# A decoder layer on one core: the search's branch behind the searches, masks one after another, gating spread over ScalarE and GpSimd

## The chip, the core and the metric

The kernel runs on one core of a Trainium2 chip. A core has a matrix engine (TensorE, PE in the profile, with its weight loads shown apart as PEld), a vector engine (VectorE, DVE), an activation engine (ScalarE, ACT), a general engine (GpSimd, POOL) and a queue for transfers (SyncE, SP). Each takes its own instructions in a fixed order; they wait for each other by semaphores. The metric is the device time of one execution in microseconds (us).

## The reference, cut to what matters

One layer of a decoder, 1024 positions of 1024 channels, in float32. The norm of x is projected by W_in; its columns are shared by two mixers, whose outputs are normed, joined and projected by W_out; a feed-forward part of 4096 channels follows.

```python
# mixer A: 4 groups of 128 channels, chunks of 128 positions
z_u, z_v = gelu(p_u), gelu(p_v)
v = rms_norm(v by group, g_v)                  # v * (mean(v*v) + eps) ** -0.5 * g_v
out_A = u * (tril(w_s[g]) @ v_chunk + b_s[g])
# mixer B: 8 query heads of 64, 2 key heads; for each block of 128 queries
score = sum_h w[t,h] * relu(q_idx[t,h] . k_idx[s] / 8) ; non-causal scores = -inf
idx   = top_k(score, 256)                      # the keys that a query may see
o     = softmax(q . k / 8 over idx) @ v
# then
o = concat(rms_norm(out_A), rms_norm(o)) @ W_out
x = x + g1 * rms_norm(o); x = x + g2 * rms_norm(relu(h2 @ W_1) ** 2 @ W_2)
```

## The kernel before

Positions are cut into eight blocks of 128 (`NB`), the partitions of a tile. A float32 product is made of fp32r parts: `proj` runs three matmuls for each of eight slices of 128 channels, so that a projection of a block onto 512 columns is a group of 24 matmuls of 128x512 (L300 to L302) into one PSUM bank `p`.

The stages of the program are: modulation and norm of x; keys, values and index keys; for the blocks 7 to 2 the index queries and `index(b)`, which adds eight relu'd products into a score row `SC` (matmul L437, relu on ScalarE L438, sum on VectorE L441 and L442); mixer A's projections with `gating`; the query projections `q_proj`; the selection; attention with softmax; W_out; the feed-forward part.

`gating(cc, j, p)` runs 16 times, for two halves `cc` of the channels and eight blocks `j`, each one step behind its projection. ScalarE takes gelu of the 512 columns into `uv` (L505), the first 256 being u and the rest v, two groups of 128. VectorE sums the squares of each group into `ss` (L510). `rstd_of` makes the factor: scale and eps on VectorE (L98), power -0.5 on GpSimd (L99). VectorE multiplies v by the factor and by the gain row `gvb` into `vn` (L518). TensorE multiplies by the mask matrix `WM` (L519), and VectorE adds the bias and multiplies by u (L520).

The selection finds, for each of the blocks 7 to 2 (the others see at most 256 keys), the 256th largest score by bisection. `select(b)` counts in 15 steps how many 16-bit upper halves lie above a trial value. Blocks 6, 4 and 3 count with a sign on ScalarE (L597, followed by two one-column steps on VectorE, L598 and L599), 7, 5 and 2 on VectorE (L585, L587, L589). The eight largest of the lower halves among those that tie give the rest of the threshold. `search_rest` covers what these eight don't: VectorE sums a flag `more` over all blocks (L632), a matmul by `ones` sums it over the partitions (L634), VectorE copies it to an integer (L635), and a branch on VectorE (L637, L638) runs a second search if it is over zero. `mask(b)` then turns score and threshold into the row `BI` of zeros and huge values (L648 to L660: small threshold steps, compare, equals, a running sum over the ties, and two combining steps). Attention runs in units (b, group of four heads, pair of heads) in the order of the blocks `OB = (0, 7, 1, 6, 5, 4, 3, 2)`: `logits` multiplies (L704), VectorE adds `BI` and takes the extreme (L705), ScalarE takes the exponential (L708), `values` transposes and multiplies by V (L743, L729). Blocks 0 and 1 need no mask of the selection.

The order on each engine is set when the program is built: a scheduler with a simulated timeline takes, from the instructions whose inputs are ready by its own reckoning, the one with the lowest `tc.cur_priority`, which counts on from stage to stage (`stage(n)` sets it to n times 100000; the selection sets its own by `PRI`). PSUM has eight banks in three rings: `mm` with two, `tr` and `lg` with three each.

Of the kernel before, what the change touches and what calls it, by code (L numbers as in the profile page):

```python
# [16 lines left out]
OP = mybir.AluOpType  # L17
# [20 lines left out]
def trunk(ctx, tc, x, c, positions, w_ada, b_ada, g_pre_mix, w_in, g_sgu_v, w_spatial, b_spatial,  # L38
# [257 lines left out]
    def proj(p, j, wt, n, ks=range(KD)):  # L296
        h, t = hT[j // 4], (j % 4) * P
        for k in ks:
            lh, ll = h[:, 0, k, t:t + P], h[:, 1, k, t:t + P]
            T.matmul(p[:, :n], lh, wt[k][:, 0, :n], start=k == 0, stop=False)  # L300
            T.matmul(p[:, :n], lh, wt[k][:, 1, :n], start=False, stop=False)  # L301
            T.matmul(p[:, :n], ll, wt[k][:, 0, :n], start=False, stop=k == KD - 1)  # L302

# [199 lines left out]
    def gating(cc, j, p):  # L503
# [3 lines left out]
        ss = ssv[:, j, 2 * cc:2 * cc + 2]  # L507
        for i in range(2):
            v = uv[:, 256 + i * P:256 + (i + 1) * P]
            V.tensor_tensor_reduce(vn[:, i], v, v, scale=1.0, scalar=0.0, op0=OP.mult, op1=OP.add,  # L510
                                   accum_out=ss[:, i:i + 1])
        rstd_of(ss, ss, P)
        pg = p_mm()
        ya = up.tile([P, 2, P], F32, tag="ya", name=nm("ya"), bufs=2)
        for i in range(2):
            g = 2 * cc + i
            v = uv[:, 256 + i * P:256 + (i + 1) * P]
            V.scalar_tensor_tensor(vn[:, i], v, ss[:, i:i + 1], gvb[:, g * P:g * P + P], op0=OP.mult, op1=OP.mult)  # L518
            T.matmul(pg[:, i * P:(i + 1) * P], WM[:, g], vn[:, i], start=True, stop=True)  # L519
# [22 lines left out]
    def q_proj(b):  # L542
        p = p_mm()
        proj(p, b, wQ, 512)
# [4 lines left out]
    for b in OB:  # L549
        q_proj(b)  # L550
        if pend:
            last_gelu = gating(*pend.pop(0))
# [77 lines left out]
    def search_rest():  # L630
# [3 lines left out]
        T.matmul(p[:1, :1], more[:, 6:7], ones, start=True, stop=True)  # L634
        V.tensor_copy(rest, p[:1, :1])  # L635
        with tc.tile_critical():
# [6 lines left out]

    def mask(b):
        n = P * (b + 1)
        cnt, sg, kk, tf, kq, lf, top8, kd, th, lo, hi = ST[b]
        sc = score(b)
        V.tensor_copy(lo, lf)  # L648
# [4 lines left out]
        eq = up.tile([P, 1024], BF, tag="uv", name=nm("eq"), bufs=2)[:, :n]  # L653
        V.tensor_scalar(lt, sc, tf, None, op0=OP.is_lt, op1=OP.add, accum_out=cnt)
# [5 lines left out]
        V.scalar_tensor_tensor(lt, lt, -BIG, eq, op0=OP.mult, op1=OP.subtract)  # L660

    for b, pri in PRI:
        tc.cur_priority = pri
        select(b)

# [139 lines left out]
    for u, (b, grp, pair) in enumerate(units):  # L805
        if u == 3:
            search_rest()
            mask(7)
# [457 lines left out]
```

## Time and profile before

| | |
|---|---|
| median of 3 runs | 1272.2 us |
| lowest and highest run | 1265.81 and 1272.71 us |
| the profiled execution's own time | 1273.95 us |
| span of its trace | 1272.2 us |
| PE, DVE, ACT, POOL busy | 1171.3, 891.8, 644.5, 206.8 us |
| mean granted clock of TensorE | 0.959 of full speed |

A timeline row shows when an instruction started, how long it took, its engine and line, the operation, `out<-in` by the program's names, shapes and a count of equal neighbours; in brackets stands the idle time of the engine just before, and what ended it. On VectorE neighbouring small instructions overlap a little, so that a row's duration is somewhat more than the step to the next one. TensorE's rows overlap likewise: the step from matmul to matmul counts. A windows row gives for a stretch its length, the busy time and instructions of each engine, TensorE's granted clock, the share of the transfer engines and the data rate. A row of lines groups equal instructions: busy time in all and the mean of one in ns, then the idle time before them.

### The profile page before, as it was taken

What the parts mean: (1) busy time and instruction counts of PE and PEld (TensorE: products, weight loads), DVE (VectorE), ACT (ScalarE), POOL (GpSimd) and SP (SyncE); (2) the same over time, 40 slices, a digit from 0 to 9 for tenths busy, and PEclk for the clock granted to TensorE, in tenths of its full rate; (3) what the DMA queues carried; (4) which work ended last, traced back from release to release, by engine and by line L of the source; (5) the groups of instructions that cost most, each with busy time, mean ns of one, the idle gap of its engine ahead of it and who ended that gap; (6) DMA issues with size and microseconds to landing.
All of it is one profiled execution on the core that took longest, in us unless ns stands there. A gap on an engine that the chain in (4) does not pass through costs nothing.

```text
span 1272.2 us, 16825 instructions
## 1 busy us (share of the span) xinstructions
PE 1171.3 (92%) x5785; PEld 987.3 (78%) x5785; DVE 891.8 (70%) x1894; ACT 644.5 (51%) x1306; POOL 206.8 (16%) x280
## 2 busy tenths in 40 slices
PE   4889888889749999999889999999999899999997
PEld 4877677668639999878767878888888788888886
DVE  6833999987297656646898776556537846776668
ACT  4544557452327855545634555555544454445442
POOL 3675614132200000003630000000000000000001
PEclk9899999899759999989979999999999999999999
DMA  9420202010002124436404854344359355633335
GB/s 336 147 79 30 71 13 83 13 50 13 10 0 59 34 88 176 179 106 242 163 33 147 284 165 159 135 154 164 133 195 373 121 167 172 215 100 100 99 89 210
DMA packets 80240, 162.42 MB, mean 128 GB/s; under 512 B 7724, under 2 KB 32920, under 8 KB 80152
## 3 DMA queue, kind: packets, MB, share of 16 engines
q1 hardware_dynamic: 80136, 161.33, 37.7%
q8 instruction: 45, 0.74, 0.2%
q14 instruction: 43, 0.35, 0.1%
q10 hardware_dynamic: 16, 0.00, 0.0%
HBM read 119.36 MB, written 41.94 MB: 127 GB/s over the span
## 4 chain that ended last, share of the span: by engine, by line
PE 51%; DVE 12%; issue 4%; DMA 3%; ACT 1%; POOL 1%; SPq 0%; DVEq 0%; POOLq 0%; ACTq 0%
PE tr L1146 8%; PE lg L1146 8%; PE mm L1146 5%; PE mm L729 3%; PE lg L963 2%; PE lg L964 2%; PE lg L965 2%; DVE w L853 2%; PE tr L963 2%; PE tr L964 2%; PE tr L965 2%; PE tr L743 2%; PE lg L704 2%; PE mm L781 1%; PE mm L963 1%
## 5 line engine op out<-in xcount | busy, mean ns | idle before, releaser
L852 ACT ACTIVATE w<-rx 128x512 fp32r<-128x512 f32 x112 | 70.6, 630 | 148.5 <-PE lg L1146 61.2
L1146 PE MATMUL tr<-w,w 128*128 128x512 f32 x504 | 134.0, 391 | 3.8 <-DVE w L853 3.8
L1146 PE MATMUL lg<-w,w 128*128 128x512 f32 x504 | 133.7, 391 | 0.0
L300 PE MATMUL mm<-w,hT 128*128 128x512 f32 (+1 forms) x288 | 115.3, 401 | 9.8 <-ACT hT L293 3.8
L853 DVE TENSOR_TENSOR w<-rx,w 128x512 fp32r<-128x512 f32 x112 | 77.3, 690 | 58.9 <-ACT w L852 58.6
L1146 PEld LDWEIGHTS tr<-w,w 128*128 128x128 f32 x504 | 95.2, 189 | 24.0 <-DVE w L853 4.2
L302 PE MATMUL mm<-w,hT 128*128 128x512 f32 (+1 forms) x288 | 112.5, 391 | 0.9 <-POOL hT L294 0.9
L301 PE MATMUL mm<-w,hT 128*128 128x512 f32 (+1 forms) x288 | 112.5, 391 | 0.0
L1146 PEld LDWEIGHTS lg<-w,w 128*128 128x128 f32 x504 | 95.1, 189 | 19.8
L1182 POOL TENSOR_TENSOR rsf<-rsf,mhalf 128x1 f32<-128x1 f32 x8 | 6.0, 751 | 606.6 <-DVE rsf L1181 606.6
L1146 PE MATMUL mm<-w,w 128*128 128x512 f32 x336 | 94.3, 391 | 0.0
L729 PEld LDWEIGHTS mm<-VV,pT 128*128 128x128 f32 x576 | 74.3, 196 | 6.4 <-ACT pT L724 4.3
L729 PE MATMUL mm<-VV,pT 128*128 128x64 f32 x576 | 75.6, 275 | 2.9 <-ACT pT L724 2.9
L704 PE MATMUL lg<-KS,qs 128*128 128x512 f32 (+5 forms) x192 | 53.9, 394 | 24.2 <-DVE mxs L705 23.1
L300 PEld LDWEIGHTS mm<-w,hT 128*128 128x128 f32 x288 | 56.8, 197 | 21.5 <-ACT hT L293 4.0
L1146 PEld LDWEIGHTS mm<-w,w 128*128 128x128 f32 x336 | 63.2, 188 | 13.1
L853 DVE TENSOR_TENSOR w<-b,w 128x512 fp32r<-128x512 f32 x96 | 65.8, 686 | 4.5 <-ACT w L852 4.5
L302 PEld LDWEIGHTS mm<-w,hT 128*128 128x128 f32 x288 | 56.2, 195 | 10.9 <-POOL hT L294 1.2
L853 DVE TENSOR_TENSOR w<-s,w 128x512 fp32r<-128x512 f32 x56 | 38.2, 690 | 37.7 <-ACT w L852 37.7
L708 ACT ACTIVATE L<-L,mxs 128x128 f32<-128x128 f32 (+7 forms) x64 | 49.2, 770 | 30.0 <-DVE mxs L705 29.8
L301 PEld LDWEIGHTS mm<-w,hT 128*128 128x128 f32 x288 | 57.0, 198 | 8.9
L852 ACT ACTIVATE w<-b 128x512 fp32r<-128x512 f32 x96 | 59.3, 618 | 7.3 <-DMA b<-in_w_ff_dram 7.3
(356 smaller groups left out, 2969.5 us busy)
## 6 DMA issues: line engine op xcount, KB each, us to landing
rx<-x_scratch SPq DMA_DIRECT2D x56, 512.0 KB, 3.6
x_scratch<-d SPq DMA_DIRECT2D x108, 256.0 KB, 3.0
ada<-in_w_ada_dram SPq DMA_DIRECT2D x48, 512.0 KB, 6.0
raw<-in_w_ff_dram SPq DMA_DIRECT2D x32, 512.0 KB, 4.0
b<-in_w_ff_dram SPq DMA_DIRECT2D x32, 512.0 KB, 4.5
x<-in_x_dram SPq DMA_DIRECT2D x16, 512.0 KB, 5.6
raw<-in_w_in_dram SPq DMA_DIRECT2D x8, 512.0 KB, 3.5
raw<-in_w_in_dram SPq DMA_DIRECT2D x16, 256.0 KB, 2.8
```

The source lines that it names most:

```text
L300: T.matmul(p[:, :n], lh, wt[k][:, 0, :n], start=k == 0, stop=False)
L301: T.matmul(p[:, :n], lh, wt[k][:, 1, :n], start=False, stop=False)
L302: T.matmul(p[:, :n], ll, wt[k][:, 0, :n], start=False, stop=k == KD - 1)
L704: T.matmul(pl, QS[b, grp][:, q, h4 * P:(h4 + 1) * P], KS[:, grp, c0:c0 + cw], start=q == 0, stop=q == 1)
L708: ex = A.activation(L, L, AF.Exp, scale=-1.0, bias=top, accum_out=sms[:, b, h:h + 1])
L729: mm = T.matmul(po[:, o:o + 64], e[:, (si * 2 + h2) * P:(si * 2 + h2 + 1) * P], VV[:, s0 + si, grp], start=first, stop=pair == 1 and s0 + ...
L852: A.activation(hi, src, AF.Copy)
L853: eng.tensor_tensor(lo, src, hi.bitcast(F32), op=OP.subtract)
L963: ms.append(T.matmul(p, a[:, 0, k], b[:, 0, k], start=start and k == 0, stop=False, skip_group_check=more))
L964: ms.append(T.matmul(p, a[:, 0, k], b[:, 1, k], start=False, stop=False, skip_group_check=more))
L965: ms.append(T.matmul(p, a[:, 1, k], b[:, 0, k], start=False, stop=stop and k == 3, skip_group_check=more))
L1146: ms.append(T.matmul(p, x[:, qa, t * P:(t + 1) * P], y[:, qb], start=start and n == 0, stop=stop and n == 2, skip_group_check=more))
```

## The change

In the gating, the sum of squares goes to ScalarE (Square with an accumulator), and so does the multiplication by the factor (Copy with a scale for each partition). The product of v and the gain row becomes a GpSimd instruction of 128x256 in place. The factor's two steps both run on GpSimd. The bank of the mixing product comes from the ring `tr`, not from `mm`; the two mixing matmuls are written ahead of the two last VectorE steps. In the selection, `search_rest` and `mask(7)` are written directly behind the searches with a priority of their own, where they stood behind the third attention unit. The last two query projections, of blocks 3 and 2, are made in `search_rest` and ordered behind the flag's matmul. The masks are chained: the compare's predecessor tells a mask to start behind the end of the one before it.

```diff
@@ -295,11 +295,14 @@
 
     def proj(p, j, wt, n, ks=range(KD)):
         h, t = hT[j // 4], (j % 4) * P
+        first = None
         for k in ks:
             lh, ll = h[:, 0, k, t:t + P], h[:, 1, k, t:t + P]
-            T.matmul(p[:, :n], lh, wt[k][:, 0, :n], start=k == 0, stop=False)
+            mm = T.matmul(p[:, :n], lh, wt[k][:, 0, :n], start=k == 0, stop=False)
+            first = first or mm
             T.matmul(p[:, :n], lh, wt[k][:, 1, :n], start=False, stop=False)
             T.matmul(p[:, :n], ll, wt[k][:, 0, :n], start=False, stop=k == KD - 1)
+        return first
 
     def rope(t, j, nh, pool):
 
@@ -505,18 +508,20 @@
         ge = A.activation(uv, p, AF.Gelu_apprx_tanh)
         vn = up.tile([P, 2, P], F32, tag="vn", name=nm("vn"), bufs=2)
         ss = ssv[:, j, 2 * cc:2 * cc + 2]
+        v = uv[:, 256:512]
         for i in range(2):
-            v = uv[:, 256 + i * P:256 + (i + 1) * P]
-            V.tensor_tensor_reduce(vn[:, i], v, v, scale=1.0, scalar=0.0, op0=OP.mult, op1=OP.add,
-                                   accum_out=ss[:, i:i + 1])
-        rstd_of(ss, ss, P)
-        pg = p_mm()
+            A.activation(vn[:, i], v[:, i * P:(i + 1) * P], AF.Square, accum_out=ss[:, i:i + 1])
+        G.tensor_tensor(v, v, gvb[:, 256 * cc:256 * cc + 256], op=OP.mult)
+        G.tensor_scalar(ss, ss, 1.0 / P, EPS, op0=OP.mult, op1=OP.add)
+        G.tensor_tensor(ss, ss, mhalf[:, :2], op=OP.pow)
+        for i in range(2):
+            A.activation(vn[:, i], v[:, i * P:(i + 1) * P], AF.Copy, scale=ss[:, i:i + 1])
+        pg = p_tr()
         ya = up.tile([P, 2, P], F32, tag="ya", name=nm("ya"), bufs=2)
         for i in range(2):
+            T.matmul(pg[:, i * P:(i + 1) * P], WM[:, 2 * cc + i], vn[:, i], start=True, stop=True)
+        for i in range(2):
             g = 2 * cc + i
-            v = uv[:, 256 + i * P:256 + (i + 1) * P]
-            V.scalar_tensor_tensor(vn[:, i], v, ss[:, i:i + 1], gvb[:, g * P:g * P + P], op0=OP.mult, op1=OP.mult)
-            T.matmul(pg[:, i * P:(i + 1) * P], WM[:, g], vn[:, i], start=True, stop=True)
             V.scalar_tensor_tensor(ya[:, i], pg[:, i * P:(i + 1) * P], cols[:, 72 + g:73 + g],
                                    uv[:, i * P:(i + 1) * P], op0=OP.add, op1=OP.mult)
         A.activation(vn.rearrange("p a b -> p (a b)"), ya.rearrange("p a b -> p (a b)"), AF.Square,
@@ -539,14 +544,14 @@
     QT = {}
     OB = (0, 7, 1, 6, 5, 4, 3, 2)
 
-    def q_proj(b):
+    def q_proj(b, behind=None):
         p = p_mm()
-        proj(p, b, wQ, 512)
+        after(proj(p, b, wQ, 512), behind)
         QT[b] = qp.tile([P, 512], F32, tag="q", name=nm("q"), bufs=8)
         A.activation(QT[b], p, AF.Copy)
         rope(QT[b], b, 8, qp)
 
-    for b in OB:
+    for b in OB[:6]:
         q_proj(b)
         if pend:
             last_gelu = gating(*pend.pop(0))
@@ -631,8 +636,10 @@
 
         V.tensor_scalar(more[:, :6], KDS, 8.0, None, op0=OP.is_gt, op1=OP.add, accum_out=more[:, 6:7])
         p = p_tr()
-        T.matmul(p[:1, :1], more[:, 6:7], ones, start=True, stop=True)
+        flag = T.matmul(p[:1, :1], more[:, 6:7], ones, start=True, stop=True)
         V.tensor_copy(rest, p[:1, :1])
+        for b in OB[6:]:
+            q_proj(b, flag)
         with tc.tile_critical():
             r = V.value_load(rest)
             with V.If(r > 0):
@@ -641,27 +648,34 @@
                     search(BI[:, boff[b]:boff[b] + P * (b + 1)].bitcast(U16), 15, lf, cnt, kd, kk, V.drain)
                 V.drain()
 
+    masked = [None]
+
     def mask(b):
+
         n = P * (b + 1)
         cnt, sg, kk, tf, kq, lf, top8, kd, th, lo, hi = ST[b]
         sc = score(b)
-        V.tensor_copy(lo, lf)
+        first = V.tensor_copy(lo, lf)
         V.scalar_tensor_tensor(th, hi, 16, lo, op0=OP.logical_shift_left, op1=OP.bitwise_or)
 
         V.tensor_tensor(tf, th.bitcast(F32), sg, op=OP.mult)
         lt = BI[:, boff[b]:boff[b] + n]
         eq = up.tile([P, 1024], BF, tag="uv", name=nm("eq"), bufs=2)[:, :n]
+        after(first, masked[0])
         V.tensor_scalar(lt, sc, tf, None, op0=OP.is_lt, op1=OP.add, accum_out=cnt)
         V.tensor_scalar(eq, sc, tf, BIG, op0=OP.is_equal, op1=OP.mult)
         V.tensor_tensor_scan(sc, eq, eq, 0.0, op0=OP.add, op1=OP.max)
         V.tensor_scalar(cnt, cnt, float(TOPK - n), BIG, op0=OP.add, op1=OP.mult)
         V.tensor_tensor(cnt, cnt, sc[:, n - 1:n], op=OP.add)
         V.scalar_tensor_tensor(eq, sc, cnt, eq, op0=OP.is_gt, op1=OP.mult)
-        V.scalar_tensor_tensor(lt, lt, -BIG, eq, op0=OP.mult, op1=OP.subtract)
+        masked[0] = V.scalar_tensor_tensor(lt, lt, -BIG, eq, op0=OP.mult, op1=OP.subtract)
 
     for b, pri in PRI:
         tc.cur_priority = pri
         select(b)
+    tc.cur_priority = 465000
+    search_rest()
+    mask(7)
 
 
     stage(6)
@@ -803,9 +817,6 @@
     logits(0)
     stack_for(2)
     for u, (b, grp, pair) in enumerate(units):
-        if u == 3:
-            search_rest()
-            mask(7)
         if u + 1 < len(units):
             logits(u + 1)
         values(u)
```

The line numbers of the profile before move a little: of the places named below, L300, L301 and L302 become L301, L303 and L304; L437 becomes L440, L519 L522, L634 L639, L319 L322, L704 L718, L705 L719, L380 L383, and the mask's lines L648 to L660 become L658 to L671.

The first place is TensorE's order where the index ends. `lg_...<-KI` is the last product of the index scores of block 2, `mm_...<-w,hT` a projection group, `<-vn,WM` a gating's mixing product. Before:

```order
L437 MATMUL lg_1668<-KI,qs_1651 128x384 x2
L437 MATMUL lg_1674<-KI,qs_1651 128x384 x2
L437 MATMUL lg_1680<-KI,qs_1651 128x384 x2
L519 MATMUL mm_2209<-vn_2204,WM 128x128
L300 MATMUL mm_2219<-w_2060,hT_142 128x512
```

After:

```order
L440 MATMUL lg_1674<-KI,qs_1651 128x384 x2
L303 MATMUL mm_1978<-w_1732,hT_143 128x512
L304 MATMUL mm_1978<-w_1732,hT_143 128x512
L301 MATMUL mm_1978<-w_1735,hT_143 128x512
L303 MATMUL mm_1978<-w_1735,hT_143 128x512
L304 MATMUL mm_1978<-w_1735,hT_143 128x512
L440 MATMUL lg_1680<-KI,qs_1651 128x384 x2
L522 MATMUL tr_1970<-vn_1962,WM 128x128 x2
L301 MATMUL mm_2021<-w_1705,hT_143 128x512
```

Behind the last index product there were 13 projection groups to come (five of mixer A and all eight of the queries); now there are 17 (nine and eight), of which 15, with 12 pairs of mixing products among them, stand ahead of the flag.

The second place is the flag on TensorE. `more` and `ones` are its operands, `hT_143` and `hT_142` the second and first half of the positions. Before, the flag stood among the last pieces of block 0's attention:

```order
L704 MATMUL lg_3863<-KS,qs_3202 128x512 x2
L729 MATMUL mm_3224<-VV,pT_3228 128x64 x2
L683 MATMUL tr_3239<-ident,ya_3232 128x128 x4
L634 MATMUL tr_3247<-ones,more 1x1
L743 MATMUL tr_3872<-ident,L_3212 128x128
L743 MATMUL tr_3872<-ident,L_3218 128x128
L319 MATMUL tr_3884<-ident,qd_3882 128x128 x4
```

After (the 48 matmuls of the two last query projections are cut to the first and the last):

```order
L304 MATMUL mm_2659<-w_2473,hT_143 128x512
L639 MATMUL tr_3073<-ones,more 1x1
L301 MATMUL mm_3076<-w_2446,hT_142 128x512
...
L304 MATMUL mm_3109<-w_2473,hT_142 128x512
L322 MATMUL tr_3753<-ident,qd_3751 128x128 x4
L718 MATMUL lg_3761<-KS,qs_3750 128x128
```

The flag now stands behind the sixth query projection and ahead of the last two, and block 0's first transposes and logits come behind those.

The third place is the masks on VectorE, directly behind the branch. `self_` and `seli_` hold a block's search values, `SC` its scores; tiles of 1024 columns are block 7's, of 896 block 6's, of 768 block 5's, of 640 block 4's. Before, the six masks went through one another:

```order
L654 TENSOR_SCALAR BI,self_2766<-SC,self_2766 128x1024
L655 TENSOR_SCALAR eq_3844<-SC,self_2766 128x1024
L649 SCALAR_TENSOR_TENSOR seli_2757<-seli_2757 128x1
L654 TENSOR_SCALAR BI,self_2764<-SC,self_2764 128x896
L655 TENSOR_SCALAR eq_3959<-SC,self_2764 128x896
L654 TENSOR_SCALAR BI,self_2762<-SC,self_2762 128x768
L654 TENSOR_SCALAR BI,self_2760<-SC,self_2760 128x640
...
L656 SCALAR_TENSOR_TENSOR SC<-eq_3844 128x1024
```

After, from the end of mask 7 to the first softmax step of block 0:

```order
L671 SCALAR_TENSOR_TENSOR BI<-BI,eq_3736 128x1024
L658 CAST seli_2715<-self_2714 128x1
...
L665 TENSOR_SCALAR BI,self_2714<-SC,self_2714 128x896
L666 TENSOR_SCALAR eq_3975<-SC,self_2714 128x896
...
L670 SCALAR_TENSOR_TENSOR eq_3975<-SC,self_2714,eq_3975 128x896
L383 TENSOR_TENSOR qs_3750<-tr_3753,qs_3750 128x512
L671 SCALAR_TENSOR_TENSOR BI<-BI,eq_3975 128x896
L658 CAST seli_2713<-self_2712 128x1
L719 ISA L_3760,mxs<-lg_3761,BI 128x128
```

Mask 7 and then mask 6 now run whole, and both stand ahead of block 0's first softmax step; of mask 5 the first half stands between that step and block 7's first softmax step, and the masks 4 to 2 come later still.

## Rows read from the trace of the kernel before

**Rows 1.** The page's first line.

```profile
span 1272.2 us, 16825 instructions
```

**Rows 2.** Windows: three stretches; the last columns are clock, DMA share, GB/s.

```profile
135.20:245.20 110.00, 98.42 (x453) 80.49 (x453) 104.86 (x312) 65.83 (x147) 34.54 (x40) 0.95 0.14 40
...
350.00:400.00 50.00, 31.66 (x211) 27.41 (x212) 48.26 (x112) 24.02 (x46) 3.28 (x2) 0.73 0.11 30
400.00:450.00 50.00, 48.86 (x397) 46.92 (x397) 30.51 (x95) 37.86 (x83) 4.70 (x8) 1.00 0.10 29
```

**Rows 3.** Timeline of VectorE from the end of the searches on.

```profile
318.01 0.16 DVE L632 TENSOR_SCALAR_CACHE_REDUCE more<-kds 128x6 f32<-128x6 f32 x1
...
329.77 0.69 DVE L380 TENSOR_TENSOR qs<-tr,qs 128x512 fp32r<-128x512 f32 x1 [10.83 <-ACT qs L379]
...
343.34 0.15 DVE L635 CAST rest<-tr 1x1 int32<-1x1 f32 x1 [3.08 <-PE tr L634]
348.39 0.34 DVE L648 CAST seli<-self 128x1 int32<-128x1 f32 x4 [4.91 <-DVEq L636]
...
366.44 0.69 DVE L705 CUSTOM_DVE_ANT_0 L<-lg,BI 128x512 f32<-128x512 f32 x1
```

**Rows 4.** Timeline of TensorE: end of the index, block 0, block 7.

```profile
240.16 0.62 PE L437 MATMUL lg<-KI,qs 128*128 128x384 f32 x2 [0.20 <-ACT relu L438]
...
328.40 0.60 PE L319 MATMUL tr<-ident,qd 128*128 128x128 f32 x4
...
344.21 0.66 PE L729 MATMUL mm<-VV,pT 128*128 128x64 f32 x4
367.19 1.22 PE L704 MATMUL lg<-KS,qs 128*128 128x512 f32 x2 [22.32 <-DVE mxs L705]
```

**Rows 5.** Timeline of ScalarE: copies at the ends of two query projections.

```profile
317.71 0.60 ACT L546 ACTIVATE q<-mm 128x512 f32<-128x512 f32 x1 [4.84 <-PE mm L302]
323.15 0.60 ACT L546 ACTIVATE q<-mm 128x512 f32<-128x512 f32 x1 [4.84 <-PE mm L302]
```

**Rows 6.** Lines by form: VectorE's steps of mask 7, from 340 to 372.

```profile
L656 DVE TENSOR_TENSOR_SCAN SC<-eq 128x1024 f32<-128x1024 bf16 x1 | 2.3, 2292 | 0.0
...
L659 DVE SCALAR_TENSOR_TENSOR eq<-SC,self,eq 128x1024 bf16<-128x1024 f32 x1 | 1.3, 1284 | 0.0
L654 DVE TENSOR_SCALAR_CACHE_REDUCE BI<-SC,self 128x1024 bf16<-128x1024 f32 x1 | 1.3, 1278 | 0.0
L660 DVE SCALAR_TENSOR_TENSOR BI<-BI,eq 128x1024 bf16<-128x1024 bf16 x1 | 1.2, 1224 | 0.0
...
L655 DVE TENSOR_SCALAR eq<-SC,self 128x1024 bf16<-128x1024 f32 x1 | 0.8, 755 | 0.0
```

**Rows 7.** Timeline of VectorE: end of the index, a gating's steps, neighbours of GpSimd.

```profile
245.04 0.62 DVE L442 SCALAR_TENSOR_TENSOR SC<-relu,WI,SC 128x384 f32<-128x384 f32 x1
...
258.19 0.29 DVE L510 CUSTOM_DVE_ANT_0 vn<-uv 128x128 f32<-128x128 f32 x1
...
258.62 0.15 DVE L589 SCALAR_TENSOR_TENSOR self<-self 128x1 f32<-128x1 f32 x1
...
260.07 0.61 DVE L518 SCALAR_TENSOR_TENSOR vn<-uv,ssv,gvb 128x128 f32<-128x128 f32 x2
...
263.23 0.35 DVE L520 SCALAR_TENSOR_TENSOR ya<-mm,cols,uv 128x128 f32<-128x128 f32 x1
...
276.59 0.94 DVE L599 SCALAR_TENSOR_TENSOR self<-self 128x1 f32<-128x1 f32 x1
277.46 2.72 DVE L518 SCALAR_TENSOR_TENSOR vn<-uv,ssv,gvb 128x128 f32<-128x128 f32 x2
```

**Rows 8.** Timeline of GpSimd at the last two rows of that.

```profile
276.22 3.81 POOL L222 TENSOR_TENSOR w<-raw,w 128x512 fp32r<-128x512 f32 x3
```

**Rows 9.** Lines by form, whole run: GpSimd and ScalarE operations of 128x256.

```profile
L294 POOL TENSOR_TENSOR hT<-hf,hT 128x256 fp32r<-128x256 f32 x8 | 6.1, 760 | 3.5 <-DVE hf L291 1.8 <-ACT hT L293 1.7
...
L522 ACT ACTIVATE vn<-ya 128x256 f32<-128x256 f32 x16 | 6.7, 416 | 5.2 <-DVE ya L520 5.2
```

## The prediction

> **What bounds the kernel now.** I read the windows first. From 400 us on TensorE is the bound: 48.86 of 50 us busy at full clock [rows 2]. Whatever makes its work start sooner before 400 comes off the end one for one, unless other work is pushed behind 400. In the 50 us before, it is different: TensorE is busy for 31.66 at a mean clock of 0.73, and VectorE for 48.26 [rows 2]. So that stretch is VectorE's, and the timeline of VectorE tells why. The searches are over at 318.01 with the sum `more`. VectorE then stands idle for 10.83 us until 329.77, where it starts on block 0; the flag reaches it only at 343.34, behind 3.08 us of waiting for TensorE; the branch costs 4.91 us of idle time; the masks start at 348.39, and block 7's first softmax step is at 366.44 [rows 3]. TensorE, which finished the query projections at 328.40 and block 0's work at about 344.87, waits 22.32 us for that step [rows 4]. The reader is to see two holes that stand one behind the other: VectorE waits for TensorE from 318 to 330, and TensorE waits for VectorE from 345 to 367. They could lie beside each other if the flag came first.
>
> Further ahead, from 135 to 245 us, VectorE is busy for 104.86 of 110 us and TensorE for 98.42 [rows 2]: there the index sums and the searches on VectorE set the pace. TensorE's last index product is at 240.16 [rows 4], VectorE's last index sum at 245.04 [rows 7].
>
> **Behind the flag.** Call F the time at which TensorE runs the flag's matmul. The steps that follow are all in VectorE's order: copy and branch, from 343.34 to 348.39, 5.05 us [rows 3]. Mask 7: the five wide steps take 2.29, 1.28, 1.28, 1.22 and 0.76, together 6.83 [rows 6]; five one-column steps stand in the chain as well, most hidden behind their neighbours, for which I take 0.7: 7.5. Mask 6 has 896 columns, seven eighths of 6.83 is 6.0, with the small steps and one subtraction of block 0 of 0.69 [rows 3] in it about 7.2. So VectorE is through at F+19.8. Meanwhile TensorE makes the two last query projections, 5.44 us each by the step between their copies [rows 5], until F+10.9; it then has only block 0's first transposes and logits, so a hole of some 8 us remains on TensorE.
>
> Block 0 then runs as before: from VectorE's start on it at 329.77 to where VectorE began to wait for the flag, 343.34 less 3.08, is 10.5 us [rows 3]. The first half of mask 5, some 3 to 4 us of VectorE, stands in this piece; the old piece was full of waits, so I let it hide. That gives block 7's first softmax step at F+30.3, with 27 as the low bound (block 0's first logits and transposes already lie behind the masks) and 33 as the high one (the mask 5 work doesn't hide). What VectorE still owes to the later masks at that point is about the same as before: there, the compares of all masks were done, here the running sum of mask 5 is done instead. So I give nothing back later.
>
> **Where F falls.** F is set by TensorE. A matmul of a group takes 5.44 / 24 = 0.227 us [rows 5]. Behind the last index product there are now 15 groups ahead of the flag, 360 matmuls, 81.8 us, and 12 pairs of mixing products of about 0.3, 3.6 us: 85.4. Before, 13 groups, 70.9 us, and some 2 us of mixing products took from 240.8 to 328.4, 87.6 us [rows 4], so 15 us were lost in waits and low clock there. Much of that was the bank of the mixing product, which stood in the ring of two that the projections use and was let go only when VectorE, busy with searches, had done L520. With the bank in another ring I take 6 us of loss for the new stretch. So F is 91.4 us behind the last index product.
>
> That product comes earlier by what VectorE is relieved of, since VectorE is the bound of that stretch. A gating had on VectorE two sums of squares, 0.43 (258.19 to 258.62), two scalings, 0.61, and one factor step of about 0.15 [rows 7]. By the old order eleven gatings had their sums of squares and ten their scalings ahead of 245.04, of sixteen; now all this is off VectorE: 11 x 0.43 + 10 x 0.6 = 10.7 us. By the new order also some four to five gatings stand behind the index that stood ahead of it, each with a pair of L520, of 0.35 each and overlapped, about 0.5 [rows 7]: 2.3. Together 13 us off.
>
> Against this stands GpSimd's new product of v and the gain. No row has it; the nearest is another 128x256 product there, 0.76 us [rows 9]. Its price for VectorE is shown by a row: while three GpSimd products of 128x512 ran for 3.81 us from 276.22 on, a one-column step that takes 0.15 otherwise took 0.94, and a pair of scalings that takes 0.61 took 2.72 [rows 7, 8]. About seven of the new products fall into the stretch. The low bound is nothing (each falls into an instruction that isn't held), the high one 7 x 0.76 = 5.3 us; a VectorE instruction in the middle of such a product waits for half of it on average, 2.7 us, which I take, as the squares and scalings that were held worst are gone from VectorE.
>
> The Trainium skill ("SBUF — State Buffer", section "🔬 SBUF: two separate sides") says that GpSimd and certain VectorE instructions share a pair of ports under an exclusive lock and that the later one blocks fully until the other is done. The stretched rows at 276 us agree. By this rule alone all sixteen products would cost VectorE 12 us, and the gain on VectorE would be nearly used up; by the rows the cost is about half, because only an instruction already at the door is held.
>
> ScalarE gets four instructions for each gating. The nearest row is a square of 128x256, 0.416 us, with its accumulator read [rows 9]; two of half the width and two copies I estimate at 1.2 us, seven times 1.2 is 8 us on 65.83 of 110 [rows 2]. It has room on the mean; in its order they stand among the index relus and the signs.
>
> So the last index sum moves from 245 to 245 - 13 + 2.7, about 234.5 (range 230 to 245), TensorE's last index product to about 229.5, and F to 229.5 + 91.4 = 321. A second way agrees: TensorE does the same work ahead of F as it did ahead of 328.40, less two projections, so with equal waits F would be 328.4 - 10.9 = 317.5; it gets more waits during the index, where 23 us of projections no longer fill its holes, and fewer behind. VectorE is not what F waits for: it was ready at 318 and is relieved of all 16 gatings, 16 x 1.04 = 17 us, of which locks take back about 6, while the searches with signs, whose ScalarE now also has the squares, may lose up to 10: ready between 307 and 317.
>
> **The sum.** Block 7's first step at 321 + 30.3 = 351.3 instead of 366.44: 15.1 us earlier. The profiled execution took 1273.95 us with a span of 1272.2 [rows 1]; less 15.1 this is 1258.9. The median of the runs is 1.75 us below that execution; the lowest of them lies 6 us below the median, so I don't shift for it: 1259.
>
> **The rivals.** A stronger one: the index ends at 230 on VectorE and TensorE loses only 2 us in the stretch behind. Then F is 225.5 + 87.4 = 313, and with 27 us behind it block 7 starts at 340, 26 us earlier: 1248. For it speaks that VectorE's load was the whole delay; against it that TensorE still has all its work.
>
> No change: the index ends where it did, as the locks take 5 us and ScalarE's squares and copies, which wait for one another and for GpSimd's power within a gating, hold up the relus that stand behind them. Then F is 240.5 + 91.4 = 332, and block 7 starts at 362: 4 us earlier, 1270, which is within 0.5%, that is 6.4 us, about what runs of this kernel can tell. For it speaks that ScalarE's order is strict and that the profile shows waits of TensorE for relus even now (0.20 at the last index product [rows 4]); against it the 44 us of room on ScalarE.
>
> Slower: ScalarE becomes the bound of the index. Its copies in a gating wait for the square, the factor and the power on GpSimd, with the product of 0.76 ahead of them there, and every relu behind them waits too; TensorE's ring of three index banks then runs full. This decides from the point where F + 30.3 passes 366.4, so F 336, the last index product at 244.7 and VectorE's last sum at 249. If it ends at 251 and the 15 us of old waits stay, F is 246.5 + 85.4 + 15 = 347, block 7 at 377, 11 us later: 1285.
>
> **How the numbers follow.** Forecast (F between 314 and 329, gain of 7 to 22 us, 1252 to 1267): 0.60. Stronger: 0.12. No change: 0.20. Slower: 0.08. The range leaves out the slower case and the far ends, and goes from the stronger case's time less a little to that of no change: 1245 to 1270. Faster by over 0.5% means under 1265.8: the stronger case and nearly all of the forecast, with a twentieth taken from it for the part with F over 327 and a little of the no-change case given back, 0.72. Within: 0.20. Slower: 0.08.
>
> **What would show it.** In the trace after: the last index sum on VectorE near 234 and not 245; the flag near 321 with no bank waits in the stretch ahead of it; an idle VectorE ahead of the flag's copy, which shows that TensorE sets F; the two last query copies within 12 us behind the flag; mask 7 in one piece of 7 to 8 us; block 7's first step 27 to 33 us behind the flag; TensorE idle some 8 us between the last query projection and block 0 instead of 22 ahead of block 7; from 400 on the same picture, 15 us earlier. Stretched one-column steps on VectorE beside the gain products would show the lock. The prediction is wrong if the index ends at 245 or later, if VectorE and not TensorE is late at the flag, or if block 7's wait for its mask returns as a wait of equal length in block 0 or in the blocks behind.

## The result, and the profile after

The changed kernel takes 1255.84 us (median of 6 runs, 1254.35 to 1258.13); the one before took 1271.49 on the same chip. The ratio is 0.9888, with an interval of 0.9863 to 0.9912: faster by 1.1%, 15.7 us. The profiled execution took 1255.87 us, 18.1 less than the profiled one before.

First the windows of the changed kernel: length, busy time of PE, PEld, DVE, ACT and POOL, then TensorE's clock, DMA share and GB/s.

```profile
135.20:245.20 110.00, 94.48 (x409) 76.37 (x408) 104.67 (x281) 78.42 (x202) 40.04 (x54) 0.88 0.13 38
160.00:190.00 30.00, 21.19 (x81) 16.13 (x80) 29.93 (x78) 18.99 (x44) 2.33 (x4) 0.74 0.00 1
...
350.00:400.00 50.00, 46.18 (x338) 42.31 (x338) 43.80 (x124) 35.79 (x76) 4.27 (x7) 0.93 0.16 48
400.00:450.00 50.00, 50.00 (x400) 48.34 (x399) 27.37 (x84) 36.08 (x74) 2.91 (x5) 1.00 0.06 17
```

Against [rows 2]: the stretch from 350 to 400 now has TensorE busy for 46 us instead of 32. From 135 to 245 TensorE does less than before, and from 160 to 190 it is starved, at a clock of 0.74. The kernel before did more there:

```profile
160.00:190.00 30.00, 26.77 (x127) 22.40 (x126) 29.86 (x98) 18.23 (x42) 5.51 (x6) 0.94 0.04 14
```

The timeline of VectorE of the changed kernel, at the points of [rows 3] and [rows 7]: last index sum, end of the searches, flag's copy, start of mask 7, first softmax steps of block 0 and of block 7.

```profile
224.20 1.30 DVE L445 SCALAR_TENSOR_TENSOR SC<-relu,WI,SC 128x384 f32<-128x384 f32 x1
...
306.68 0.15 DVE L637 TENSOR_SCALAR_CACHE_REDUCE more<-kds 128x6 f32<-128x6 f32 x1
...
316.47 0.15 DVE L640 CAST rest<-tr 1x1 int32<-1x1 f32 x1 [8.88 <-PE tr L639]
325.43 0.15 DVE L658 CAST seli<-self 128x1 int32<-128x1 f32 x1 [8.81 <-DVEq L643]
...
341.15 0.28 DVE L719 CUSTOM_DVE_ANT_0 L<-lg,BI 128x128 f32<-128x128 f32 x1
...
348.60 0.69 DVE L719 CUSTOM_DVE_ANT_0 L<-lg,BI 128x512 f32<-128x512 f32 x1 [0.20 <-PE lg L718]
```

Block 7 starts at 348.60 instead of 366.44, 17.8 us earlier. The end of the index came 20.8 us earlier and the end of the searches 11.3; but VectorE then stood idle for 8.88 us until TensorE reached the flag, and for 8.81 in the branch, where it had been 4.91.

TensorE's timeline has the last index product, the flag, and the hole that is left behind the last query projection:

```profile
221.06 0.52 PE L440 MATMUL lg<-KI,qs 128*128 128x384 f32 x2
...
316.24 0.19 PE L639 MATMUL tr<-ones,more 128*1 128x1 f32 x2
...
340.23 0.91 PE L718 MATMUL lg<-KS,qs 128*128 128x128 f32 x3 [8.77 <-DVE qs L383]
```

The 22.32 us of [rows 4] have become 8.77, ahead of block 0, where masks 7 and 6 stand on VectorE.

### The profile page after: what moved, and what is told of

It is laid out like the page before. It is cut to its first block, busy times and chain, and to the rows that moved or that the text cites. A ratio compares the mean times of both kernels' runs of the same rounds, so it can differ in the third digit from the quotient of the medians.

```text
span 1254.1 us, 16871 instructions
## 1 busy us (share of the span) xinstructions
PE 1169.4 (93%) x5785; PEld 987.7 (79%) x5785; DVE 876.2 (70%) x1782; ACT 661.9 (53%) x1402; POOL 222.9 (18%) x312
## 4 chain that ended last, share of the span: by engine, by line
PE 60%; DVE 7%; issue 3%; DMA 1%; POOL 1%; ACT 1%; DVEq 0%; POOLq 0%; SPq 0%; ACTq 0%
PE lg L1157 9%; PE tr L1157 9%; PE mm L1157 6%; PE mm L743 5%; PE lg L974 3%; PE lg L975 3%; PE lg L976 3%; PE tr L974 3%; PE tr L976 3%; PE tr L975 3%; PE tr L757 2%; PE lg L718 2%; PE mm L974 2%; PE mm L975 2%; PE mm L976 2%
## 5 line engine op out<-in xcount | busy, mean ns | idle before, releaser
L301 PE MATMUL mm<-w,hT 128*128 128x512 f32 (+1 forms) x288 | 113.2, 394 | 7.9 <-ACT hT L293 3.4
L304 PE MATMUL mm<-w,hT 128*128 128x512 f32 (+1 forms) x288 | 111.4, 388 | 1.0 <-POOL hT L294 1.0
L303 PE MATMUL mm<-w,hT 128*128 128x512 f32 (+1 forms) x288 | 111.7, 388 | 0.0
L301 PEld LDWEIGHTS mm<-w,hT 128*128 128x128 f32 x288 | 56.2, 195 | 18.6 <-ACT hT L293 3.6
L304 PEld LDWEIGHTS mm<-w,hT 128*128 128x128 f32 x288 | 55.7, 194 | 10.4 <-POOL hT L294 1.3
L303 PEld LDWEIGHTS mm<-w,hT 128*128 128x128 f32 x288 | 56.2, 195 | 8.5
L718 PE MATMUL lg<-KS,qs 128*128 128x512 f32 (+5 forms) x192 | 53.3, 388 | 10.2 <-DVE qs L383 8.8
```

The lines of the kernel that those rows point to most:

```text
L301: mm = T.matmul(p[:, :n], lh, wt[k][:, 0, :n], start=k == 0, stop=False)
L718: T.matmul(pl, QS[b, grp][:, q, h4 * P:(h4 + 1) * P], KS[:, grp, c0:c0 + cw], start=q == 0, stop=q == 1)
```

## The experiments

Theory A: TensorE sets the flag; its work ahead of it is the same whatever VectorE does in the index, so the place of the flag pays, and the relief of VectorE little. Theory B: the relief in the gating pays. Diffs are against the changed kernel unless they say otherwise.

### e1: the selection's part alone

The whole body of `gating` is that of before; of its lines:

```diff
-            A.activation(vn[:, i], v[:, i * P:(i + 1) * P], AF.Square, accum_out=ss[:, i:i + 1])
-        G.tensor_tensor(v, v, gvb[:, 256 * cc:256 * cc + 256], op=OP.mult)
...
+        rstd_of(ss, ss, P)
+        pg = p_mm()
...
+            V.scalar_tensor_tensor(vn[:, i], v, ss[:, i:i + 1], gvb[:, g * P:g * P + P], op0=OP.mult, op1=OP.mult)
```

> The selection's part alone (flag ahead of the last two query projections, masks chained), with the gating of before. Theory A: TensorE sets the flag, its work ahead of it is the same whatever VectorE does in the index, so the flag falls at about 328.4 - 10.9 = 317.5, VectorE is ready for it at about 318, and block 7's first softmax step follows 32 us later at about 350: 1257 us, nearly all of the gain. Theory B: the relief of VectorE by the gating is what pays, since it moves the end of the index by 20 us: then this part alone gains under 5 us, 1267 or more.

1257.54 us, ratio 0.9892 (0.9862 to 0.9922). VectorE's timeline:

```profile
244.89 0.61 DVE L445 SCALAR_TENSOR_TENSOR SC<-relu,WI,SC 128x384 f32<-128x384 f32 x1
...
319.33 0.15 DVE L635 TENSOR_SCALAR_CACHE_REDUCE more<-kds 128x6 f32<-128x6 f32 x1
...
328.74 0.15 DVE L656 CAST seli<-self 128x1 int32<-128x1 f32 x1 [8.42 <-DVEq L641]
...
352.57 0.69 DVE L717 CUSTOM_DVE_ANT_0 L<-lg,BI 128x512 f32<-128x512 f32 x1
```

The index ends where it ended before [rows 7], and the gain is there all the same. So theory A holds on what pays. That TensorE sets the flag holds here only just: both engines come to it at nearly the same time, and TensorE waits 0.64 us for VectorE's sum.

```profile
319.63 0.19 PE L637 MATMUL tr<-ones,more 128*1 128x1 f32 x2 [0.64 <-DVE more L635]
```

The medians of e1 and of the changed kernel differ by 1.7 us and their intervals overlap: what the gating adds to the selection's part here is not clear of noise.

### e2: the gating's part alone

The kernel before, with the changed kernel's body of `gating`: e1's diff turned round, in the other kernel.

> The gating's part alone, with the selection of before. Theory A: the index ends some 20 us earlier on VectorE, but the flag still stands behind all eight query projections and block 0, which TensorE reaches only 1 to 3 us earlier, so 1268 to 1271 us. Theory B: 10 us or more are gained, 1261 or less.

1269.28 us, ratio 1.0003 (0.9986 to 1.0019): no change, within what A gave. In VectorE's timeline the index ends at 223.25, but the flag is copied at 339.42 and block 7 starts at 362.52:

```profile
223.25 1.30 DVE L442 SCALAR_TENSOR_TENSOR SC<-relu,WI,SC 128x384 f32<-128x384 f32 x1
...
339.42 0.15 DVE L637 CAST rest<-tr 1x1 int32<-1x1 f32 x1 [3.04 <-PE tr L636]
...
362.52 0.67 DVE L707 CUSTOM_DVE_ANT_0 L<-lg,BI 128x512 f32<-128x512 f32 x1
```

Of 21.8 us at the end of the index, 3.9 are left at block 7. The ratio of the runs shows none of these 3.9, and its interval leaves room for 1.8 us. The traced execution, 1263.40 us, is the shortest of the ten, so its trace need not stand for the median; where the 3.9 us went in the others is not shown.

### e3: the last query projections behind the branch

On TensorE's order of the changed kernel the branch's block begins 20 matmuls behind the flag:

```
1029 L303 MATMUL mm_3076<-w_2470,hT_142 128x512
1030 L1273 UNCONDITIONAL_BRANCH
1031 L304 MATMUL mm_3076<-w_2470,hT_142 128x512
```

```diff
         V.tensor_copy(rest, p[:1, :1])
-        for b in OB[6:]:
-            q_proj(b, flag)
...
         after(first, masked[0])
+        firsts[b] = first
...
     search_rest()
     mask(7)
+    for b in OB[6:]:
+        q_proj(b, firsts[7])
```

> The changed kernel with the last two query projections tied behind the first step of mask 7 instead of behind the flag, so that none of their matmuls stands on TensorE between the flag and its end of the block that the branch opens (20 did). Theory A: the branch waits for every engine to end what stands ahead of it, so the 8.8 us of idle VectorE fall to about 4.9 and the time by about 4 us, to 1252. Rival: the 8.8 us are the fetch of instructions behind a jump over more code, or the price of an idle engine; then they stay and so does the time, 1256.

1249.21 us, ratio 0.9844 (0.9814 to 0.9873). VectorE's timeline:

```profile
316.30 0.15 DVE L640 CAST rest<-tr 1x1 int32<-1x1 f32 x1 [8.88 <-PE tr L639]
321.42 0.15 DVE L657 CAST seli<-self 128x1 int32<-128x1 f32 x1 [4.97 <-DVEq L641]
...
344.04 0.68 DVE L721 CUSTOM_DVE_ANT_0 L<-lg,BI 128x512 f32<-128x512 f32 x1
```

The flag falls at the same time, and the idle time in the branch is 4.97 again: 3.8 us are the wait for TensorE's 20 matmuls (20 x 0.227 = 4.5 us behind the flag). The waits themselves stand in the traces, as semaphore instructions of VectorE's queue at the block's entry; shown are their count (those at the program's end among them) and their shortest, middle and longest time in ns, first in the changed kernel, then in e3:

```profile
L1273 DVEq EVENT_SEMAPHORE  x8: 21/50/4024, 316.9 to 1254.1; - x8
```

```profile
L1275 DVEq EVENT_SEMAPHORE  x8: 21/50/50, 316.7 to 1243.8; - x8
```

One wait of 4.02 us is gone. In the changed kernel it ends at 321.28, and TensorE's 20th matmul behind the flag, which starts at 320.84 and takes 0.39, ends at 321.23; in e1 the two ends are 324.64 and 324.60. So theory A holds, and the rival, by which the 8.8 us would have stayed, does not. Block 7 starts 4.6 us earlier, and the medians differ by 6.6; no run of the one kernel reaches into those of the other.

### e4: mask 6 behind block 0

`behind` is block 0's last softmax step (L719). Every mask called from the attention gets it; as the masks are chained, mask 6 is the one that it moves:

```diff
-    def mask(b):
+    def mask(b, behind=None):
...
         after(first, masked[0])
+        after(first, behind)
...
-            mask(MASKS[u])
+            mask(MASKS[u], LR[3])
```

> The changed kernel with mask 6 tied behind block 0's last softmax step; all else as it is. Theory A: TensorE's wait of 8.8 us in block 0 is the wait for mask 6, and vanishes; block 7's first softmax step comes about 7 us earlier, and TensorE, being the bound from there on, keeps it: 1249. Rival: mask 6 then lies between block 7's softmax steps, where VectorE is nearly full, and the 7 us come back there: 1255 to 1257.

1257.17 us, ratio 0.9900 (0.9869 to 0.9931): the rival. Block 0 started at 333.96, as soon as TensorE had its logits, and block 7 at 344.30, 4.3 us earlier; but mask 6 then stood between its softmax steps on VectorE:

```profile
351.66 0.74 DVE L720 CUSTOM_DVE_ANT_0 L<-lg,BI,mxs 128x512 f32<-128x512 f32 x1
...
352.33 1.14 DVE L671 SCALAR_TENSOR_TENSOR eq<-SC,self,eq 128x896 bf16<-128x896 f32 x1
353.39 0.73 DVE L720 CUSTOM_DVE_ANT_0 L<-lg,BI,mxs 128x512 f32<-128x512 f32 x1
```

### e5, e9, e10: five projections ahead of the flag, and the masks' order

e5 is e3 with `OB[:5]` and `OB[5:]`. e9 also ties mask 5 behind block 0's last softmax step, e10 also mask 6 behind the softmax of block 0's first unit.

> As e3 (last query projections tied behind mask 7's first step), and only five query projections ahead of the flag, three behind it. Theory A (TensorE sets the flag, VectorE was ready at 306.7): the flag falls one projection earlier, near 311, the masks start near 316, block 0's first softmax step near 331 to 332, where TensorE's last query projection (still near 328) takes over as the bound; block 7's first softmax step 2 to 3 us earlier than in e3, 1246 to 1247 us. Rival: the flag is not what counts any more once the branch no longer waits, and the time is that of e3, 1249.

> As e5, and mask 5 tied behind block 0's last softmax step. In e5 block 0's first logits were ready at 327 on TensorE, mask 6 was done at 331.1, but the first half of mask 5 stood ahead of the softmax until 334.9. Theory A: VectorE's order is what holds block 0 there; its first softmax step comes at 331, block 7's near 340.5 instead of 344.0, 1247 to 1249 us. Rival (as e4 showed for mask 6): the mask comes back between block 7's softmax steps, and the time is that of e5, 1251 to 1252.

> As e9, and mask 6 tied behind the softmax of block 0's first unit only, so that it runs in the gaps of block 0 and not behind it as in e4. Theory A: block 0 starts near 327.5, as soon as TensorE has its logits, and mask 6 fills VectorE's gaps: block 7's first softmax step near 338 to 340, 1246 to 1248 us. Rival: what is put off lies between block 7's steps and comes back, 1250 to 1253.

e5: 1251.53 us, 0.9859 (0.9832 to 0.9887), no gain on e3. The flag came 6 us earlier, at 310.25, and block 7 where it was. VectorE's timeline shows why: the new order has the first half of mask 5 ahead of block 0.

```profile
310.25 0.14 DVE L640 CAST rest<-tr 1x1 int32<-1x1 f32 x1 [3.44 <-PE tr L639]
315.16 0.15 DVE L657 CAST seli<-self 128x1 int32<-128x1 f32 x1 [4.77 <-DVEq L641]
...
333.25 1.76 DVE L667 TENSOR_TENSOR_SCAN SC<-eq 128x768 f32<-128x768 bf16 x1
334.93 0.27 DVE L721 CUSTOM_DVE_ANT_0 L<-lg,BI 128x128 f32<-128x128 f32 x1
...
344.00 0.69 DVE L721 CUSTOM_DVE_ANT_0 L<-lg,BI 128x512 f32<-128x512 f32 x1
```

e9: 1251.68 us, 0.9866 (0.9826 to 0.9905). Block 0 started at 332.04 and block 7 at 341.92, 2.1 us earlier than in e5, and the time doesn't show it: the rival, or too little to measure. e10: 1246.69 us, 0.9826 (0.9796 to 0.9856). Block 0 started at 326.13, held by TensorE and not by a mask, and block 7 at 335.38, with mask 6 among block 0's steps:

```profile
326.13 0.29 DVE L723 CUSTOM_DVE_ANT_0 L<-lg,BI 128x128 f32<-128x128 f32 x1 [3.66 <-PE lg L722]
...
335.38 0.68 DVE L723 CUSTOM_DVE_ANT_0 L<-lg,BI 128x512 f32<-128x512 f32 x1
```

The time is theory A's. The intervals of e10, e9 and e3 overlap, so that the order of the masks is worth something beside e3 rests on the traces and not on the medians.

### e6: e3 with the gating of before

> As e3, but with the gating of before: prices the gating's part beside a branch that doesn't wait. Theory A: VectorE is ready for the flag only at 319.3 as in e1, some 3 us behind the 316.3 of e3, so block 7's first softmax step is some 3.5 us later than in e3, 1252 to 1253 us. Rival: the gating's part is worth nothing, as e2 against before says: 1249.

1254.56 us, 0.9869 (0.9845 to 0.9893). Block 7 started at 346.72, 2.7 us later than in e3; the medians differ by 5.4 (the ratios by 0.25%, 3.2 us), but the two intervals overlap. Once the branch doesn't wait, the gating's part seems worth something, which is not clear of noise; A had 3.5 us.

### e7: the mixing product's bank in the ring of the projections again

```diff
-        pg = p_tr()
+        pg = p_mm()
```

> The changed kernel with the mixing product's bank from the ring mm again. Theory A: the projections wait again for VectorE's last gating step, as before (6.7 to 9 us of such waits), the flag comes 3 to 8 us later, 1259 to 1264 us. Rival: that step comes soon enough now that the rest of the gating is off VectorE: 1256.

1258.97 us, 0.9909 (0.9884 to 0.9934): near A's number, but not by A's way: TensorE's waits for VectorE's last gating step came to 2.4 us, and the flag was copied at 312.50, 4 us earlier than in the changed kernel. The edit changed the order: only ten projection groups instead of fifteen are left between the last index product and the flag, the index ended at 246.25, and TensorE was at the flag at 305.5, 11 us earlier than in the changed kernel. It had been kept busy from 160 to 190; then it waited for VectorE's `more`, and its clock fell. A window of e7:

```profile
160.00:190.00 30.00, 25.81 (x116) 21.43 (x116) 29.46 (x76) 21.43 (x58) 8.23 (x11) 0.89 0.04 14
```

TensorE's timeline at the flag:

```profile
312.26 0.19 PE L639 MATMUL tr<-ones,more 128*1 128x1 f32 x2 [6.75 <-DVE more L637]
...
312.97 0.63 PE L303 MATMUL mm<-w,hT 128*128 128x512 f32 x1
313.39 0.63 PE L304 MATMUL mm<-w,hT 128*128 128x512 f32 x1
```

VectorE's, with the branch, the first half of mask 5 and the first steps of blocks 0 and 7, and below it the waits at the block's entry:

```profile
323.62 0.15 DVE L658 CAST seli<-self 128x1 int32<-128x1 f32 x1 [10.83 <-DVEq L643]
...
341.51 1.75 DVE L667 TENSOR_TENSOR_SCAN SC<-eq 128x768 f32<-128x768 bf16 x1
343.18 0.27 DVE L719 CUSTOM_DVE_ANT_0 L<-lg,BI 128x128 f32<-128x128 f32 x1
...
349.68 0.65 DVE L719 CUSTOM_DVE_ANT_0 L<-lg,BI 128x512 f32<-128x512 f32 x1
```

```profile
L1273 DVEq EVENT_SEMAPHORE  x8: 21/50/5971, 313.0 to 1256.5; - x8
```

After 6.75 us of waiting a matmul steps by 0.42 us instead of 0.227, the granted clock being 0.50 from 312.2 to 317. The 20 matmuls that the branch waits for took longer by that, and so did the branch: 10.83, of which the longest wait is 5.97; it ends at 319.41, the 20th matmul at 319.36. That alone doesn't make e7 slower, since its masks still start 1.8 us earlier than in the changed kernel. But its order has the first half of mask 5 ahead of block 0, as in e5, so that block 0 starts 2.0 us later and block 7 1.1 us later.

### e8: no branch

`search_rest` without its flag and its branch.

> The changed kernel without the second search: no flag, no branch (its output is the same where the flag is zero). Theory A: the masks run while TensorE makes the query projections, block 0 starts when these end, near 328, block 7's first softmax step near 338 instead of 348.6, and the time is 1245 to 1247; the rest against e3 is the price of the jump itself. Rival: the masks' 30 us of VectorE then delay the later searches, whose masks come late instead, and the time is that of e3 or above, 1249 to 1256.

1246.62 us, 0.9810 (0.9787 to 0.9833): A's number, but not by A's way. Block 7 started only at 349.55, since the scheduler spread the masks through the searches, which then ended at 334.00, as the rival had it; but from there to the last logits of the attention it took 172.4 us instead of 179.3, with VectorE rid of its masks. The second search's flag and branch, with the order of masks that they force, are 9.2 us of the changed kernel's time; e3 wins 6.6 of them back with the branch in, and e10 all.

### e11: no gain product

```diff
-        G.tensor_tensor(v, v, gvb[:, 256 * cc:256 * cc + 256], op=OP.mult)
```

> The changed kernel without the product of v and the gain row on GpSimd (the gain is left out of the computation). Theory A: the product delays VectorE through the shared port by 2 us at most in the whole index, and TensorE sets the flag anyway: the last index sum within 1.5 us of 224.2, the flag's copy within 1 us of 316.5, 1254 to 1257 us. Rival (each product holds VectorE for its whole 0.84 us, and the chain through GpSimd delays ScalarE): 6 us or more earlier at the last index sum, and 1250 or less.

1249.99 us, 0.9841 (0.9813 to 0.9869). The last index sum came at 223.69, 0.5 us earlier: the products hardly held VectorE. But the flag's copy came at 313.74, 2.7 us earlier. The first row is a window of the changed kernel, the second the same window of e11:

```profile
221.00:245.00 24.00, 19.38 (x91) 15.86 (x90) 23.40 (x79) 16.84 (x48) 13.51 (x15) 0.95 0.35 101
```

```profile
221.00:245.00 24.00, 22.17 (x105) 18.20 (x104) 23.47 (x73) 15.97 (x47) 13.05 (x15) 1.00 0.36 105
```

TensorE was busy for 2.8 us more there. In the changed kernel it waited at 242.31 for a gating's scaled values (L518 on ScalarE, behind the power on GpSimd) for 3.04 us, and its clock from 245 to 270 was 0.91; in e11 it waited for them for 1.13 at most, and the clock was 1.00. How the 2.7 us at the flag divide between the wait and the clock is not shown. The time is the rival's, and so is the chain through GpSimd; on VectorE A was right. The two profiled executions, 1255.87 and 1253.27, differ by 2.6 us, which is what the flag won; the rest of the 5.9 us between the medians does not stand in these traces.

### e12: e7's bank, e3's tie, e10's masks

> The bank of e7 (ring mm), with e3's tie of the last two query projections and e10's order of the masks, six query projections ahead of the flag. Theory A: with e7's order TensorE is not starved in the index and reaches the flag near 305.5, where it waits for VectorE until about 312; the branch no longer waits for the 20 matmuls (11.1 us in e7, about 5 here), the masks start near 317.5, block 0's first softmax step is near 325.5, block 7's near 335: 1244 to 1247 us, as fast as e10 though the index ends 20 us later. Rival: the end of the index counts for itself, and this one is slower than e10 by 5 us or more, 1252.

1244.55 us, ratio 0.9802 (0.9782 to 0.9821), the fastest of all, though not clear of e10. VectorE's timeline:

```profile
246.62 0.61 DVE L445 SCALAR_TENSOR_TENSOR SC<-relu,WI,SC 128x384 f32<-128x384 f32 x1
...
312.31 0.13 DVE L640 CAST rest<-tr 1x1 int32<-1x1 f32 x1
317.45 0.15 DVE L657 CAST seli<-self 128x1 int32<-128x1 f32 x1 [4.85 <-DVEq L641]
...
336.11 0.69 DVE L723 CUSTOM_DVE_ANT_0 L<-lg,BI 128x512 f32<-128x512 f32 x1
```

The index ends 22 us later than in the changed kernel, and block 7 starts 12.5 us earlier. When the index ends is no measure of the time by itself: behind the last index product TensorE has ten projection groups left here ahead of the flag, and 15 in the changed kernel.

## Why the prediction was right

**The end, and its mechanism.** 1259 was forecast and 1255.84 measured, with block 7's first step at 351.3 forecast and 348.60 found. That the two holes would fall beside each other is what e1 shows: the selection's part alone gives the gain. That the sum came within 3 us is in part luck. The flag was 4.8 us earlier than taken and block 0 3.05 us shorter, the piece from the flag to the masks 4.1 us longer and the masks 1.0 us.

**The end of the index: mis-sized by half.** Forecast 234.5, measured 224.2. The relief was larger than taken, and the term for GpSimd's locks, 2.7 us, too large. The lines by form, up to the end of the index, give 8.4 us for the scalings L518, 7.8 for the squares L510 with their accumulators, 3.5 for nine L520 that now stand behind it, and 2.0 for the step below: 21.7 together, overlaps not taken off, where I had 13. First of before, then of after, the one-column step that the searches on ScalarE use:

```profile
L599 DVE SCALAR_TENSOR_TENSOR self<-self 128x1 f32<-128x1 f32 x20 | 5.2, 260 | 0.1
```

```profile
L604 DVE SCALAR_TENSOR_TENSOR self<-self 128x1 f32<-128x1 f32 x19 | 3.2, 167 | 0.1
```

Its mean fell from 260 to 167 ns. Before, three of these steps took 0.51, 0.93 and 1.18 us, each while GpSimd ran products of 128x512 (L222); after, none took more than 0.28. GpSimd's lines for the same two stretches show that fewer of those products lie there:

```profile
L222 POOL TENSOR_TENSOR w<-raw,w 128x512 fp32r<-128x512 f32 x10 | 13.7, 1395 | 0.8 <-ACT w L221 0.8
```

```profile
L222 POOL TENSOR_TENSOR w<-raw,w 128x512 fp32r<-128x512 f32 x4 | 6.0, 1502 | 3.2 <-ACT w L221 3.2
```

So these 2 us go with the place of the L222 products and not with the steps that the gating gave up. The rule of the Trainium skill ("SBUF — State Buffer", section "🔬 SBUF: two separate sides") is borne out where a product of the gain did meet such a step, which took 0.66 us instead of 0.15 and ended with the product:

```profile
235.42 0.66 DVE L604 SCALAR_TENSOR_TENSOR self<-self 128x1 f32<-128x1 f32 x1
```

```profile
235.32 0.74 POOL L514 TENSOR_TENSOR uv<-uv,gvb 128x256 f32<-128x256 f32 x1
```

But only those that meet pay. Six gain products ran up to the end of the index, where I had taken seven, and e11 puts their sum at 0.5 us; the high bound, a whole product each, had been 5.3.

**The flag: right by its second way.** Forecast 321 by the index and 317.5 by TensorE's work; measured 316.24. The sum used the first way, and that was wrong in both its terms: the index product came at 221, 8 us earlier than taken, and 95 us lay between it and the flag instead of 91.4. Its link was wrong too. It held 15 projection groups fixed behind the index product, but their number goes with the order: 15 in the changed kernel, 11 in e1, ten in e7. In e1 the index product is at 240.01, from which the first way would put the flag at 331; it ran at 319.63. The relief of the gating moves projections from ahead of the index product to behind it, and the flag only by the 3.4 us between e1 and the changed kernel. The early index was bought by leaving TensorE without projections (26.77 to 21.19 us busy in the 30 us from 160 on), and e7, with a late index, had TensorE at the flag 11 us sooner. The waits for the bank (L520) are gone from TensorE's list as forecast.

**From the flag to block 7.** Forecast 30.3 us, measured 32.4 from the flag at 316.24. The branch took 3.9 us more than taken: I carried over the 5.05 of [rows 3], though TensorE's order has the branch's block 20 matmuls behind the flag (where the dots stand in the order shown ahead of the prediction); that the block waits for TensorE's queue I had not seen. The masks took 15.7 instead of 14.7 us; block 0 7.45 instead of 10.5, with the first half of mask 5 in it: VectorE waited there for 0.5 us in all, where the old piece had 5 us of waits. The hole on TensorE is 8.77 us where some 8 were forecast.

**Nothing given back later**: held; from block 7's first step to the last logits of the attention it is 179.3 us after and 177.9 before.

**The rivals.** No change and slower needed an index that ends at 245 or later to cost time; e1, with 244.89, and e12, with 246.62, show that it needn't. The slower case had ScalarE as the bound of the index, with its end at 249 or later; with 78.42 us of 110 on ScalarE it ended at 224.2.

## What to carry to other kernels

When a step of one engine waits for a step of another, count the work that stands ahead of it on the engine that is waited for; relief of the engine that waits moves only its own idle time. A branch on one engine can wait for another's queue: look in the order for what stands between the value it tests and the branch on each engine. Work that is put off is free only where the engine has gaps (e10), and comes back where it is full (e4).

## What was not expected of the hardware

The branch cost 4.8 to 5.0 us of VectorE's idle time where TensorE had no projection queued ahead of it (e3, e5, e10, e12), 8.4 to 8.8 with 20 matmuls of TensorE at full clock ahead, and 10.83 with 20 at a clock that began at 0.50 (e7). Of the 5 us that are left in e3, 3.0 lie on VectorE's queue between its last compare, at 318.1, and the next instruction, at 321.1; what they are spent on is not shown.

Behind the attention there is a stretch in which TensorE waits for VectorE and its clock falls, and by how much differs from trace to trace: the 40 us that begin 80 us behind the last logits of the attention, first in the trace before, then in e1's.

```profile
624.30:664.30 40.00, 31.72 (x127) 25.37 (x126) 39.27 (x51) 16.94 (x33) 19.31 (x14) 0.83 0.18 65
```

```profile
615.20:655.20 40.00, 31.41 (x137) 25.04 (x135) 39.27 (x51) 16.84 (x32) 18.29 (x13) 0.91 0.18 67
```

From the last logits to the end these two traces take 727.9 and 722.2 us. That a part of the scatter of some 5 us between runs of one kernel lies there too is likely but not shown, since each kernel has one trace. Of the runs of the kernel before that were taken beside e9, three with a mean clock of 0.966 or 0.967 took 1266.91 to 1269.77 us, and two with 0.956 and 0.958 took 1272.31 and 1272.38. Why the clock differs stays open.
